# Attention of a hybrid decoder layer as one hand-ordered sequence, with the softmax factors applied to the products and the sums of the down weights moved behind later tiles

## The chip, the core and the metric

One Trainium2 chip, one NeuronCore. The metric is the device time of the whole program in microseconds (us). Engines are TensorE (PE; its weight loads are shown as PEld), VectorE (DVE), ScalarE (ACT), GpSimd (POOL) and SyncE (SP), which here issues all DMAs. Every engine takes its instructions in the order of its own program; a semaphore wait holds back all that is queued behind it on that engine.

## The reference, cut to what matters

A layer of a decoder trunk: T = 1024 tokens, 1024 channels, float32. One input projection feeds three groups of heads (convolution, sparse attention, RWKV-7). Their outputs are concatenated, projected and added to the residual; a gated MLP with a short convolution follows. The change lies in attention, which for 8 query heads (2 groups g of 4 heads r) sums three softmax branches with a sigmoid gate for each. With 16 blocks in all and the best 16 chosen, the selected branch is causal attention over all keys.

```python
def masked_softmax(s, mask, axes):
    s = jnp.where(mask, s, NEG_INF)
    m = jnp.max(s, axis=axes, keepdims=True)
    e = jnp.where(mask, jnp.exp(s - m), 0.0)
    return e / jnp.maximum(jnp.sum(e, axis=axes, keepdims=True), TINY)
...
        o_cmp = jnp.einsum('bgrqn,bngd->bqgrd', pc.astype(v_cmp.dtype), v_cmp)
        o_sel = jnp.einsum('bgrqnl,bgqnld->bqgrd', ps.astype(vg.dtype), vg)
        o_win = jnp.einsum('bgrqk,bkgd->bqgrd', pw.astype(vwc.dtype), vwc)
        return gc[..., 0:1] * o_cmp + gc[..., 1:2] * o_sel + gc[..., 2:3] * o_win
```

## The kernel before

**Stages.** The program normalises x, transposes it, projects it in the three groups, runs convolution, RWKV and attention, then the output projection (out_tile), the MLP's first half (ffn_up) and its second (ffn_down), both as Strassen-like products of half matrices. The code is traced in program order, and a planner that models times then fixes the order of every engine's instructions ahead of the run: of those that are ready it takes the one with the highest priority, which is program order, except that the RWKV steps (start, solve, chain in build) are raised far above all else. Tiles of one tag share a fixed number of buffers (table B, line 23 on), and a tile waits until its buffer is free.

**RWKV.** Four units (j, h), j a pair of heads and h half of the tokens. For each, rwkv_prep and rwkv_mats make the operands and solve a triangular system by substitution on GpSimd, 31 dependent steps of two instructions (L528, L530); rwkv_solve finishes the inverse on TensorE, and rwkv_chain walks over eight chunks with the state (L591, L596, L609, L611) and ends with a store to the DRAM buffer md (L638). The order is "... S10 C01 V10 S11 C10 V11 C11": the operands of unit 11 are made after the solve of unit 10 and the chain of unit 11 is last. Units 10 and 11 fall beside attention.

**Attention.** Query tiles of 128 tokens in the order 7, 6, 5, 4, 0, 3, 2, 1 (attn_tile, L821). For each: loads of Q through SP; scores against the compressed keys (L839), their softmax with two GpSimd steps (L849, L857); then for branch 2 (window, W = up to 640 keys) and branch 1 (selected, W = (i+1) * 128) and for each of four heads r a unit of work, for both groups g:

- score products in pieces of up to 512 keys into PSUM banks of the tag mm, 3 of them (L893, L894: high and low part of the keys);
- a VectorE instruction that adds the mask, copies to SBUF (tile pp) and finds the minimum of the negated scores (L897); L902 joins the minima of two pieces;
- exponential with sums on ScalarE (L904), reciprocal of the sum (L905), times the gate (L906), and the scaling of the probabilities by that factor on VectorE (L911, two for each unit);
- transposes of 128 x 128 blocks into a bank of the tag tr, four blocks or, at the odd end, two (L918), a ScalarE copy to SBUF (pT, L921), and AV products into halves of 64 columns of the array (L926). All three branches accumulate into one bank (av), which L932 copies out and L933 stores.

A pp buffer holds 1280 columns (pk=1280): one unit of 640 keys, both groups, takes one of six buffers; units of more keys take two.

**Sums of down weights.** down_sums(f) (L936) loads four 128 x 512 blocks of w_down, forms four differences on GpSimd (L945 to L948) and stores them for ffn_down. It is called for 11 values of f behind the tiles, two a tile, with nothing to hold the instructions to that place.

**Behind attention.** wout_load (L954) brings w_out in 16 blocks, split into high and low parts; most of the buffers for it are those that RWKV and the keys leave. out_tile(i) (L977) loads two mixed tiles from md (L984; the first holds the convolution and RWKV channels, the second those of attention), splits them (L120, L121) and makes 2 x 24 products (L229), from tile 7 down to tile 0.

## Time and profile before

| what | value |
|---|---|
| median of three runs | 1516.3 us (1515.09 to 1518.08) |
| profiled execution | 1516.71 us, of it 1515.0 us span between first and last instruction |
| granted TensorE clock, mean | 0.962 |
| TensorE busy | 1418.2 us of the span (94%) |
| VectorE, ScalarE, GpSimd busy | 1001.0, 684.0, 500.2 us |
| attention, first score product to last copy | about 400 to 733 us |

The profile is one execution. A duration of a TensorE instruction includes its way through the array, and instructions overlap, so what one costs in a row of others is read from the distance of starts. A wait is put down to the instruction that came last. The views used are the table of stretches, the waits, the list of groups by line, the instructions of one line, and the timeline.

### The profile page before, as it was taken

The numbers are of one execution on the slowest core, as the hardware profiler recorded it, in microseconds if no ns is written. First come the engines' busy times: TensorE is split into PE (matmuls) and PEld (weight loads), VectorE is DVE, ScalarE is ACT, GpSimd is POOL, SyncE is SP. The second block draws the span as 40 slices with busy tenths as digits, with TensorE's granted clock in tenths as the row PEclk, the third lists the DMA queues.
The fourth block names the chain that finished last, engine by engine and source line by source line (L and its number), as shares of the span: only waits on it lengthen the run. The fifth ranks groups of instructions, "written<-read, shape, count | busy, mean of one in ns | idle before, by whom it ended". The sixth has DMA issues, their size and how long they took to land.

```text
span 1515.0 us, 22973 instructions
## 1 busy us (share of the span) xinstructions
PE 1418.2 (94%) x8025; PEld 1128.7 (75%) x8025; DVE 1001.0 (66%) x2171; ACT 684.0 (45%) x1361; POOL 500.2 (33%) x607
## 2 busy tenths in 40 slices
PE   6999688999798999999599899999999999999997
PEld 5887566777666777767478677888888788888886
DVE  5346696454488587777446776775876876666675
ACT  5432255534155665776333353333333443445463
POOL 1003887910487204100000133453453443113310
PEclk9999887999699999999899999999999999999999
DMA  6133223434888301310742113332332333986633
GB/s 184 36 105 80 46 77 95 146 89 119 246 259 270 101 21 41 81 43 16 226 121 84 57 56 98 105 112 84 104 119 91 104 104 111 383 295 213 207 91 111
DMA packets 206680, 186.71 MB, mean 123 GB/s; under 512 B 56355, under 2 KB 145764, under 8 KB 206564
## 3 DMA queue, kind: packets, MB, share of 16 engines
q1 hardware_dynamic: 206564, 185.24, 39.5%
q8 instruction: 63, 1.03, 0.3%
q14 instruction: 53, 0.43, 0.1%
HBM read 126.99 MB, written 58.20 MB: 122 GB/s over the span
## 4 chain that ended last, share of the span: by engine, by line
PE 78%; DVE 10%; DMA 4%; POOL 2%; issue 2%; ACT 2%; SPq 1%; DVEq 0%; ACTq 0%; POOLq 0%
PE mm L229 13%; PE gb L229 12%; PE rw L229 10%; PE ga L229 8%; PE gc L229 8%; PE tr L229 5%; PE tr L918 4%; PE av L926 4%; PE mm L893 2%; PE mm L894 2%; POOL sx L528 1%; PE rw L493 1%; POOL sT L530 1%; DVE pp L897 1%; DVE pp L911 1%
## 5 line engine op out<-in xcount | busy, mean ns | idle before, releaser
L229 PE MATMUL mm<-hT,whi 128*128 128x512 f32 x608 | 201.6, 413 | 0.0
L229 PE MATMUL mm<-hT,wlo 128*128 128x512 f32 x304 | 126.1, 416 | 18.8 <-DVE wlo L121 18.8
L229 PEld LDWEIGHTS mm<-hT,whi 128*128 128x128 f32 x608 | 118.3, 197 | 28.5 <-issue 1.4
L921 ACT ACTIVATE pT<-tr 128x512 f32<-128x512 f32 (+1 forms) x152 | 79.8, 536 | 62.1 <-PE tr L918 59.0
L926 PE MATMUL av<-pT,V 128*64 128x128 f32 x1056 | 96.4, 289 | 1.3 <-ACT pT L921 1.1
L279 POOL TENSOR_TENSOR cacc<-cacc,ctap 128x512 f32<-128x512 f32 x60 | 91.6, 1550 | 15.0 <-ACT ctap L278 14.9
L229 PE MATMUL rw<-woh,mix 128*128 128x512 f32 x240 | 79.4, 406 | 17.0 <-ACT mix L120 17.0
L918 PE MATMUL tr<-idn,pp 128*128 128x128 f32 x528 | 91.6, 292 | 0.5 <-DVE pp L911 0.3
L121 DVE TENSOR_TENSOR sp<-rb,sp 128x512 fp32r<-128x512 f32 x66 | 57.1, 865 | 50.4 <-ACT sp L120 50.3
L1072 POOL TENSOR_TENSOR S<-wraw,wr 128x512 f32<-128x512 f32 x22 | 28.5, 1295 | 181.0 <-DVE or L107 79.2
L229 PEld LDWEIGHTS mm<-hT,wlo 128*128 128x128 f32 x304 | 59.9, 197 | 37.0 <-DVE wlo L121 20.1
L893 PE MATMUL mm<-KH,QS 128*128 128x512 f32 (+2 forms) x192 | 77.3, 407 | 10.0 <-DVE mx L897 7.7
L229 PE MATMUL rw<-sp,sp 128*128 128x512 f32 x330 | 86.1, 389 | 0.0
L229 PE MATMUL tr<-sp,sp 128*128 128x512 f32 x330 | 85.9, 389 | 0.0
L926 PEld LDWEIGHTS av<-pT,V 128*64 128x64 f32 x1056 | 59.9, 138 | 27.3 <-issue 13.0
L528 POOL TENSOR_TENSOR sx<-sN,sT 128x60 f32<-128x60 f32 (+24 forms) x124 | 47.4, 382 | 97.4 <-DMA sN<-dn 90.5
L918 PEld LDWEIGHTS tr<-idn,pp 128*128 128x128 f32 x528 | 56.5, 142 | 30.0 <-issue 27.9
L120 ACT ACTIVATE sp<-rb 128x512 fp32r<-128x512 f32 x66 | 41.6, 630 | 74.0 <-PE tr L229 37.5
L121 DVE TENSOR_TENSOR sp<-b,sp 128x512 fp32r<-128x512 f32 x88 | 68.8, 789 | 5.3 <-ACT sp L120 5.1
L229 PEld LDWEIGHTS rw<-sp,sp 128*128 128x128 f32 x330 | 62.0, 188 | 12.8
L229 PEld LDWEIGHTS tr<-sp,sp 128*128 128x128 f32 x330 | 62.0, 188 | 12.8
L904 ACT ACTIVATE pp<-pp,nm 128x640 f32<-128x640 f32 (+3 forms) x64 | 57.6, 904 | 23.7 <-DVE nm L902 22.1
(457 smaller groups left out, 3721.0 us busy)
## 6 DMA issues: line engine op xcount, KB each, us to landing
wraw<-in_ffn_w_up_dram SPq DMA_DIRECT2D x44, 256.0 KB
wr<-in_ffn_w_gate_dram SPq DMA_DIRECT2D x44, 256.0 KB
pdS<-prod SPq DMA_DIRECT2D x44, 256.0 KB
b<-pdS SPq DMA_DIRECT2D x44, 256.0 KB
rb<-tdT SPq DMA_DIRECT2D x44, 256.0 KB
pdA<-prod SPq DMA_DIRECT2D x33, 256.0 KB
b<-pdA SPq DMA_DIRECT2D x33, 256.0 KB
wraw<-in_w_in_dram SPq DMA_DIRECT2D x30, 256.0 KB
```

The source lines that it names most:

```text
L120: self.nc.scalar.activation(hi, src, AF.Copy)
L121: getattr(self.nc, eng).tensor_tensor(lo, src, hi.bitcast(F32), op=ALU.subtract)
L229: mm = lambda l, r, **k: self.nc.tensor.matmul(out, l, r, skip_group_check=more, **k)
L279: nc.gpsimd.tensor_tensor(t[:, o:o + 512], t[:, o:o + 512], z, op=ALU.add)
L528: v_.tensor_tensor(x, N[:, q, q + 1:32].unsqueeze(2).to_broadcast([P, n, w]), Tm[:, q, 0:w].unsqueeze(1).to_broadcast([P, n, w]), op=ALU.mult)
L893: pe.matmul(pts[g][:, 0:n], QS[:, r, g, :], KH[g][hf][:, ks], start=True, stop=False)
L894: pe.matmul(pts[g][:, 0:n], QS[:, r, g, :], KL[g][hf][:, ks], start=False, stop=True)
L904: s.activation(Ps[g], Ps[g], AF.Exp, bias=nm[:, g:g + 1], scale=-1.0, accum_out=sm[:, g:g + 1])
L918: pe.transpose(pt[:, o:o + P], Ps[g][:, kt * P:kt * P + P], self.idn)
L921: s.activation(pT[:, 0:n], pt[:, 0:n], AF.Copy)
L926: pe.matmul(av[g * 64:g * 64 + 64, r * P:r * P + P], self.V[kk // 2][:, kk % 2, vo + g * 64:vo + g * 64 + 64], pT[:, o:o + P], start=first ...
L1072: gp.tensor_tensor(t, x, y, op=op)
```

## The change

Attention of all tiles becomes one function (attention) that writes out TensorE's order. self.pe gives each attention instruction of TensorE an ordering edge, without a semaphore, to the one before it, so that the planner keeps them in that order; instructions of other parts may still come between them. Work goes in rounds of two items. An item is four transposes of blocks that may belong to two units ("k"), the transposes of the compressed probabilities ("c"), or those of the factors ("f"). A round is: the transposes of its items with their copies, the AV products of the round before, the end of a branch where one is due, scores of the next round's units, scores of the units of the round after that while pp buffers are left, and the compressed AV product.

The probabilities stay unscaled. When all four units of a branch have their sums, attn_factors makes gate over sum for 128 x 8 values, copies each over 64 columns, four transposes bring that into the layout of the products, and VectorE multiplies the branch's products by it (out of the av bank) and adds them to a sum in SBUF that begins with the compressed branch's product. The compressed branch has a bank of its own (mm). Every fourth pT copy is made by VectorE (dvc=4).

There are 9 pT buffers instead of 5. A pp buffer holds 1024 columns instead of 1280, so that a unit of 640 keys takes two. down_sums are called when a tile is opened (its first scores are issued), 0, 3, 2, 3, 2, 1, 0, 0 of them, and their GpSimd instructions are ordered behind the last GpSimd step (formerly L857) of that tile's compressed branch.

```diff
-                      QS=2, pp=6, q8=2, pT=5, xn=8, ds=((0, 1), (2, 3), (4, 5), (6, 7), (8, 9), (10,), (), ()), h2=14, graw=2, prod=5, ft=4, u=4, wr2=4, wfh=3, wfl=3, S=2, p1=2, om=6, grow=2, pre=2, ap=(), wf=("own", "wf", "om"), hd=("vector",) * 4, tq=((0, 1, 2, 3),), ttag=("tr", "rw"),
-                      mm=3, tr=2, av=1, rw=2, mm1=2, tr1=2, pm=2, early="00 01", ga=2, gb=1, gc=1, y=16, r4=15, ta=3, tb=4, mid=2, de=dict(S3="gpsimd", T3="vector", T1="gpsimd", T2="gpsimd", T4="vector", S1="gpsimd", S2="gpsimd", S4="gpsimd"), order=(7, 6, 5, 4, 0, 3, 2, 1), sc=0, pk=1280, st="sync", last=5, sub="gpsimd",  steps="lora r0 S00 conv taps V00 S01 keys q C00 V01 r1a cmp0 r1b cmp1 r1c S10 C01 V10 S11 C10 V11 C11", both=0, cm="gpsimd", rpu=(), wo="vector", tap=(0, 31), vt="cv", vs="vector", va={1: (0, 1), 3: (2, 3), 5: (4, 5), 7: (6, 7)}, vq="sync", vl=1, vw=1, t1=("pm", "tr1"), into={6: (6, 2), 4: (4, 2), 3: (3, 1), 2: (2, 1), 1: (1, 1), 0: (0, 1)})
+                      QS=2, pp=6, q8=2, pT=9, dvc=4, xn=8, ds=((), (0, 1, 2), (3, 4), (5, 6, 7), (8, 9), (10,), (), ()), h2=14, graw=2, prod=5, ft=4, u=4, wr2=4, wfh=3, wfl=3, S=2, p1=2, om=6, grow=2, pre=2, ap=(), wf=("own", "wf", "om"), hd=("vector",) * 4, tq=((0, 1, 2, 3),), ttag=("tr", "rw"),
+                      mm=3, tr=2, av=1, rw=2, mm1=2, tr1=2, pm=2, early="00 01", ga=2, gb=1, gc=1, y=16, r4=15, ta=3, tb=4, mid=2, de=dict(S3="gpsimd", T3="vector", T1="gpsimd", T2="gpsimd", T4="vector", S1="gpsimd", S2="gpsimd", S4="gpsimd"), order=(7, 6, 5, 4, 0, 3, 2, 1), sc=0, pk=1024, st="sync", last=5, sub="gpsimd",  steps="lora r0 S00 conv taps V00 S01 keys q C00 V01 r1a cmp0 r1b cmp1 r1c S10 C01 V10 S11 C10 V11 C11", both=0, cm="gpsimd", rpu=(), wo="vector", tap=(0, 31), vt="cv", vs="vector", va={1: (0, 1), 3: (2, 3), 5: (4, 5), 7: (6, 7)}, vq="sync", vl=1, vw=1, t1=("pm", "tr1"), into={6: (6, 2), 4: (4, 2), 3: (3, 1), 2: (2, 1), 1: (1, 1), 0: (0, 1)})
...
-        cm.tensor_tensor(C4, C4, each(sm), op=ALU.mult)
+        self.cm_ins = cm.tensor_tensor(C4, C4, each(sm), op=ALU.mult).ins
...
+    def pe(self, *a, transpose=False, **k):
+
+        ins = (self.nc.tensor.transpose if transpose else self.nc.tensor.matmul)(*a, **k)
+        if self.pe_last is not None:
+            self.tc.add_manual_dep(ins.ins, self.pe_last.name, mybir.DependencyInfo(mybir.DependencyClass.NoSync, mybir.DependencyReason.DATA),
+                                   reason="attention")
+        self.pe_last = ins.ins
+        return ins
...
-                v.reciprocal(sm, sm)
-                v.tensor_tensor(sm, sm, gt[:, r:8:4, br], op=ALU.mult)
-                for g in range(2):
-                    if g < self.B["sc"]:
-                        s.activation(Ps[g], Ps[g], AF.Copy, scale=sm[:, g:g + 1])
-                    else:
-                        v.tensor_scalar(Ps[g], Ps[g], sm[:, g:g + 1], None, op0=ALU.mult)
...
+    def attn_T(self, x, units):
+
+        pt = self.bank("tr")
+        y = [(units[n], kt, g) for n, kt in x for g in range(2)]
+        for n, (u, kt, g) in enumerate(y):
+            self.pe(pt[:, n * P:n * P + P], u.Ps[g][:, kt * P:kt * P + P], self.idn, transpose=True)
+        pT = self.xt([P, 512], "pT")
+        self.ncopy += 1
+        if self.B["dvc"] and self.ncopy % self.B["dvc"] == 0:
+            self.nc.vector.tensor_copy(pT, pt)
+        else:
+            self.nc.scalar.activation(pT, pt, AF.Copy)
+        return [(*z, pT[:, n * P:n * P + P]) for n, z in enumerate(y)]
+
+    def attn_factors(self, t, br):
+
+        nc = self.nc
+        F = t.sums[br]
+        nc.vector.reciprocal(F, F)
+        f2 = F.rearrange("p (r g) -> p g r", g=2)
+        nc.vector.tensor_tensor(f2, f2, t.gt[:, :, br].rearrange("p (g r) -> p g r", g=2), op=ALU.mult)
+        X = self.xt([P, 512], "pT", name="fx")
+        nc.vector.tensor_copy(X.rearrange("p (a b) -> p a b", b=64), F.unsqueeze(2).to_broadcast([P, 8, 64]))
+        t.X[br] = X
...
+    def attention(self, order, done_tile):
...
+                rounds += [items[k:k + 2] for k in range(0, len(items), 2)]
+        rounds.append([("f", len(units) - 1)])
+
+        top = [max([u for z, x in it if z == "k" for u, _ in x], default=-1) for it in rounds]
...
+        def cmp_av(t):
+            cav = self.bank("mm")
+            self.pe(cav, self.vcmp[0:t.n2], t.ct[0:t.n2], start=True, stop=True)
+            t.mix = self.xt([P, 512], "pT", name="mix")
+            s.activation(t.mix, cav, AF.Copy)
+
+        def fac_T(t, br):
+            pt = self.bank("tr")
+            for r in range(4):
+                self.pe(pt[:, r * P:r * P + P], t.X[br][:, r * P:r * P + P], self.idn, transpose=True)
+            t.fs = self.xt([P, 512], "pT", name="fs")
+            s.activation(t.fs, pt, AF.Copy)
+
+        def end(t, br):
+            v.tensor_tensor(t.fs, t.av, t.fs, op=ALU.mult)
+            v.tensor_tensor(t.mix, t.mix, t.fs, op=ALU.add)
+            if br == 1:
+                self.st.dma_start(self.md[:, 4:8, t.i * P:t.i * P + P], t.mix.rearrange("p (r q) -> p r q", q=P))
+        issue(top[1])
+        late = []
+        for k, items in enumerate(rounds):
...
+            self.attn_AV(late)
+            late = done
+            for u in fs:
+                end(u.t, u.br)
+            far = top[min(k + 2, len(rounds) - 1)]
+            near = top[min(k + 1, len(rounds) - 1)]
+            issue(near)
+            while opened[0] <= far and used() + (1 if 2 * units[opened[0]].w * P <= self.B["pk"] else 2) <= self.B["pp"]:
+                issue(opened[0])
+            for t in cs:
+                cmp_av(t)
...
-        for n, i in enumerate(order):
-            self.attn_tile(i)
-            for f in self.B["ds"][n]:
-                self.down_sums(f)
+        ds = iter(self.B["ds"])
+
+        def done_tile():
+            for f in next(ds):
+                with self.tc.issue_after(self.cm_ins):
+                    self.down_sums(f)
+        self.attention(order, done_tile)
```

## Rows read from the trace of the kernel before

**Rows 1.** Table of stretches: us, each engine's busy us (instructions), granted clock, DMA share, GB/s.

```profile
400.00:500.00 100.00, 89.09 (x656) 65.65 (x657) 79.12 (x231) 50.04 (x100) 78.18 (x106) 0.90 0.83 262
500.00:613.00 113.00, 112.53 (x1051) 85.63 (x1050) 82.11 (x292) 72.59 (x153) 26.66 (x74) 1.00 0.15 39
613.00:733.00 120.00, 117.58 (x1106) 86.15 (x1105) 88.08 (x370) 86.13 (x228) 4.32 (x8) 1.00 0.20 53
...
740.00:750.00 10.00, 3.03 (x7) 2.48 (x8) 2.08 (x3) 2.44 (x4) 0.00 (x0) 0.50 1.04 329
```

**Rows 2.** TensorE's waits from 400 to 500: who waits for whom: us, times, longest.

```profile
PE mm L893 <- DVE mx L897: 7.4, 6, 2.5
```

**Rows 3.** Instructions of L528 (404:504, 585:612) and L596 (500:733): ns min/median/max, first and last start.

```profile
L528 POOL TENSOR_TENSOR sx<-sN,sT x31: 202/289/730, 404.7 to 502.3; 128x60 f32<-128x60 f32 x3, 128x28 f32<-128x28 f32 x2, 128x54 f32<-128x54 f32 x2, 128x48 f32<-128x48 f32 x2
...
L528 POOL TENSOR_TENSOR sx<-sN,sT x31: 203/285/428, 585.9 to 610.4; 128x60 f32<-128x60 f32 x3, 128x28 f32<-128x28 f32 x2, 128x54 f32<-128x54 f32 x2, 128x48 f32<-128x48 f32 x2
...
L596 PE MATMUL rw<-VA,KB x30: 269/273/276, 590.9 to 716.0; 128*128 128x128 f32 x30
```

**Rows 4.** Timeline of GpSimd from 404 us: start, us, line, form, [idle before].

```profile
407.26 1.29 POOL L945 TENSOR_TENSOR wraw<-whi,wraw 128x512 f32<-128x512 f32 x1 [0.39 <-DVE mx L897]
408.51 0.26 POOL L530 TENSOR_TENSOR sT<-sT,sx 128x28 f32<-128x28 f32 x1
408.72 1.28 POOL L946 TENSOR_TENSOR whi<-wlo,whi 128x512 f32<-128x512 f32 x1
```

**Rows 5.** Timelines of SP's queue and of TensorE behind attention.

```profile
736.02 0.43 SPq L638 DMA_DIRECT2D md<-gz  x1
...
741.14 0.43 SPq L984 DMA_DIRECT2D mix<-md  x1
...
746.97 0.80 PE L229 MATMUL rw<-woh,mix 128*128 128x512 f32 x1 [13.32 <-ACT mix L120]
...
764.18 0.50 PE L229 MATMUL rw<-woh,mix 128*128 128x512 f32 x1 [2.48 <-ACT mix L120]
```

**Rows 6.** Timeline of TensorE, 600 to 608 us; neighbours of one line are merged.

```profile
601.01 0.39 PE L894 MATMUL mm<-KL,QS 128*128 128x512 f32 x1
601.24 0.28 PE L893 MATMUL mm<-KH,QS 128*128 128x256 f32 x1
...
605.98 0.44 PE L918 MATMUL tr<-idn,pp 128*128 128x128 f32 x2
606.34 0.66 PE L926 MATMUL av<-pT,V 128*64 128x128 f32 x8
606.93 0.66 PE L918 MATMUL tr<-idn,pp 128*128 128x128 f32 x4
607.34 0.37 PE L893 MATMUL mm<-KH,QS 128*128 128x256 f32 x1
```

**Rows 7.** Groups by line, 400 to 733: count, busy us, mean ns, idle before.

```profile
L921 ACT ACTIVATE pT<-tr 128x512 f32<-128x512 f32 (+1 forms) x152 | 79.8, 536 | 62.1 <-PE tr L918 59.0 <-issue 1.8
L911 DVE TENSOR_SCALAR pp<-pp,sm 128x640 f32<-128x640 f32 (+7 forms) x128 | 66.6, 562 | 1.3
L906 DVE TENSOR_TENSOR sm<-sm,gates 128x2 f32<-128x2 f32 x64 | 13.8, 216 | 1.2
L905 DVE RECIPROCAL sm<-sm 128x2 f32<-128x2 f32 x64 | 10.2, 160 | 17.1 <-ACT pp L904 16.8
```

**Rows 8.** Instructions of L443 and L447, RWKV steps like those the change adds.

```profile
L443 DVE COPY cum<-rrn x4: 419/423/426, 105.0 to 556.6; 128x512 f32<-128x512 f32 x4
...
L447 DVE TENSOR_TENSOR lw<-lw,rw x2: 679/684/689, 378.1 to 560.7; 128x512 f32<-128x512 f32 x2
```

**Rows 9.** VectorE's groups by line and shape, 415 to 500 and 510 to 580.

```profile
L902 DVE TENSOR_TENSOR nm<-mx 128x2 f32<-128x2 f32 x13 | 6.0, 460 | 0.1
...
L902 DVE TENSOR_TENSOR nm<-mx 128x2 f32<-128x2 f32 x10 | 1.5, 155 | 0.1
```

**Rows 10.** Groups by line and shape, 400 to 733, VectorE and ScalarE.

```profile
L897 DVE CUSTOM_DVE_ANT_0 pp<-mm,msel 128x512 f32<-128x512 f32 x48 | 32.3, 685 | 7.7 <-PE mm L894 6.0 <-PE tr L918 1.3
...
L904 ACT ACTIVATE pp<-pp,nm 128x1024 f32<-128x1024 f32 x8 | 9.1, 1142 | 4.7 <-DVE nm L902 4.7
L904 ACT ACTIVATION_READ_ACCUMULATOR pp<-pp,nm 128x1 f32 x64 | 12.2, 190 | 0.0
```

More of the change, by code (lines that the diff above doesn't have):

```diff
@@ new lines, in attn_open @@
+        self.cm_ins = cm.tensor_tensor(C4, C4, each(sm), op=ALU.mult).ins
+        t.X = {}
+        t.sums = [None] + [self.small([P, 8], "sums", bufs=6) for _ in range(2)]
+        return t
+    def pe(self, *a, transpose=False, **k):
[5 more added lines that the diff above has]
+        return ins
@@ new lines, in attn_scores, with mask, piece @@
+    def attn_scores(self, u):
+        v, s = self.nc.vector, self.nc.scalar
+        t, br, r = u.t, u.br, u.r
+        k1 = (t.i + 1) * P
+        lo_k = u.lo_k = max(0, k1 - 640) if br == 2 else 0
+        M = self.mwin if br == 2 else self.msel
+        W = u.W = k1 - lo_k
+        KH, KL = self.KH[br - 1], self.KL[br - 1]
+        pcs = [(a, b) for a, b in ((lo_k, min(k1, 512)), (max(lo_k, 512), k1)) if a < b]
+        npc = len(pcs)
+        mx = self.small([P, 2, npc], f"mx{npc}", bufs=6)
+        if 2 * W <= self.B["pk"]:
+            Pt = self.xt([P, 2, W], "pp")
+            Ps = u.Ps = [Pt[:, g, :] for g in range(2)]
+        else:
+            Ps = u.Ps = [self.xt([P, W], "pp") for _ in range(2)]
+        def mask(ka, kb):
+            e = 640 - (k1 - kb)
+            return M[:, e - (kb - ka):e] if br == 2 or kb == k1 else M[:, 0:kb - ka]
+        def piece(c):
+            ka, kb = pcs[c]
+            hf, n = ka // 512, max(kb - ka, 256)
+            o = min(ka % 512, 512 - n)
+            ks = slice(o, o + n)
+            pts = [self.bank("mm") for _ in range(2)]
+            for g in range(2):
+                self.pe(pts[g][:, 0:n], t.QS[:, r, g, :], KH[g][hf][:, ks], start=True, stop=False)
+                self.pe(pts[g][:, 0:n], t.QS[:, r, g, :], KL[g][hf][:, ks], start=False, stop=True)
+            o = ka % 512 - o
+            for g in range(2):
+                v.tensor_tensor_reduce(Ps[g][:, ka - lo_k:kb - lo_k], pts[g][:, o:o + kb - ka], mask(ka, kb), 1.0, 3.4e38,
+                                       ALU.add, ALU.min, mx[:, g, c:c + 1])
+            if c == npc - 1:
@@ L929, in attn_tile @@
-            if br == 2:
-                cmp_av()
-        mf = self.xt([P, 512], "pT", name="mix")
-        s.activation(mf, av, AF.Copy)
-        self.st.dma_start(self.md[:, 4:8, i * P:i * P + P], mf.rearrange("p (r q) -> p r q", q=P))
+                    s.activation(Ps[g], Ps[g], AF.Exp, bias=nm[:, g:g + 1], scale=-1.0, accum_out=t.sums[br][:, 2 * r + g:2 * r + g + 1])
+        return [lambda c=c: piece(c) for c in range(npc)]
+    def attn_T(self, x, units):
[7 more added lines that the diff above has]
+            self.nc.vector.tensor_copy(pT, pt)
+        else:
+            self.nc.scalar.activation(pT, pt, AF.Copy)
+        return [(*z, pT[:, n * P:n * P + P]) for n, z in enumerate(y)]
@@ new lines, in attn_factors, with attn_AV @@
+    def attn_factors(self, t, br):
[7 more added lines that the diff above has]
+        t.X[br] = X
+    def attn_AV(self, done):
+        for u, kt, g, pT in done:
+            t, r = u.t, u.r
+            if r == 0 and kt == 0 and g == 0:
+                t.av = self.bank("av")
+                t.first = [True, True]
+            vo = 128 if u.br == 2 else 0
+            kk = u.lo_k // P + kt
+            self.pe(t.av[g * 64:g * 64 + 64, r * P:r * P + P], self.V[kk // 2][:, kk % 2, vo + g * 64:vo + g * 64 + 64], pT,
+                    start=t.first[g], stop=r == 3 and kt == u.w - 1)
+            t.first[g] = False
```

137 lines of the change are left out of this document (73 added, 64 removed).

## The prediction, made before the changed kernel was run

> **What bounds the kernel now.** I read the table of stretches first, for where TensorE is short of work, then its waits, then GpSimd's rows and the timeline around the end of attention. Attention runs from 400 to 733 us, with what is left of the RWKV group between its instructions. From 500 to 613 TensorE is busy 112.5 us of 113, from 613 to 733 117.6 of 120, both at the full clock [rows 1]: there the order is limited by TensorE's own work. Only the first 100 us are loose: TensorE is idle for 10.9 us and its granted clock is 0.90 [rows 1], so another tenth of the time runs short, 10 us. Some 20 us are lost there. The largest wait of that stretch is for VectorE's masked copy of the scores (L897), 7.4 us [rows 2].
>
> The second thing to see is GpSimd. The serial solve of the third RWKV unit (31 steps of L528 and L530) runs from 404.7 to 503 us; the next one, with nothing beside it, from 585.9 to 611, that is 25 us [rows 3]. The difference of 73 us is down_sums: 44 subtractions of 1.28 us that take turns with the steps, one 1.29 us subtraction between two steps of 0.26 us [rows 4]. So the RWKV chain, which is serial through solve, products and the next solve, goes on to a last state product at 716.0 us [rows 3].
>
> The third is the seam behind attention. The RWKV result is stored at 736.0 us, the load of the first mixed tile, which needs it, is issued at 741.1, and TensorE starts the output projection at 747.0 after 13.3 us of idleness [rows 5]; the clock is then at the lower of its two levels (1.2 GHz, 0.50 granted from 740 to 750) [rows 1]. With 2.5 us of idleness at 764.2 [rows 5] and about 8 us of products at half speed (4 us lost) I put the seam at 13.3 + 2.5 + 4 = 20 us. So the end of attention and the end of RWKV coincide today, and both must move for a gain.
>
> **The change part by part.** *TensorE's work.* In the timeline eight AV instructions take 606.34 to 606.93, 74 ns each; four transposes 606.93 to 607.34, 103 ns each; but two transposes ahead of an AV group take 0.36 us, 0.15 more than two of 103 ns [rows 6]. So I charge 0.15 us for each visit to the AV products, which use half of the array's columns. Before there are at most 152 visits, one per pT copy [rows 7]. After it, the loop makes 83 rounds (counted from order, the widths w and two items a round) with one visit each: 69 x 0.15 = 10 us less. Added are 16 x 4 = 64 transposes of the factors, 64 x 0.103 = 6.6 us; the transposes and AV products themselves stay. Net -3 us.
>
> *VectorE.* Scaling of the probabilities (L911, 66.6 us) goes; 64 small reciprocals and products (10.2 and 13.8 us) become 16 each [rows 7], 18 us less. Added for each of 16 tile branches: a broadcast copy of 0.42, a product from PSUM of 0.68 and an addition of about the same [rows 8], 16 x 1.8 = 29 us, and every fourth pT copy, 33 x about 0.68 = 22 us (no such copy is in the trace; the nearest row is the PSUM product; the copy of 0.42 is the other end, 14 us). Net -67 - 18 + 29 + 22 = -34 us. *ScalarE:* 152 copies (79.8 us) [rows 7] become 99 plus 16 of the factors, at 0.54 us 62 us, so -18. Neither bounds 500 to 733 us, so these count only where TensorE waits for them: in the first 100 us. There L911 alone is more than the largest wait, and GpSimd's queue no longer puts subtractions ahead of the first tile's compressed scores. I take half of the 20 us, -10; the ends are 0 and -20.
>
> *The sums.* None is issued on GpSimd before the second tile is opened; then 3, 2, 3, 2, 1 follow the tiles, each 4 x 1.28 = 5.1 us [rows 4]. The 44 instructions, their loads and stores on SP's queue stay the same in number. The solve at 404.7 should take about 25 us, so it ends near 430 instead of 503; what follows it in the chain moves with it by up to 73 us. A sum that is queued ahead of a step of the last solve delays it by 1.28 us; the three sums of one tile could cost it 15 us. Both leave the RWKV end before 700 us, hidden behind attention; without that cover the seam comes back. Then the first mixed tiles can be loaded early, w_out finds its buffers, and the output projection follows attention without a gap: -20 us; ends 0 and -20. SP's loads of Q for the next tile now stand behind stores that wait for the sums; a tile lasts some 40 us and three sums 15, so I cost it at nothing.
>
> *The held order.* This is what is paid. A unit's scores are issued one round of transposes and products ahead of their use: 8 x 0.103 + 16 x 0.074 + 0.15 = 2.2 us of cover, more where the round holds other scores. A unit of 1024 keys needs eight score products of 0.23 us [rows 6], and from the last of them: a masked copy of 0.69, the minimum of 0.16 to 0.46 us [rows 9], and two exponentials of 1.14 + 0.19 on ScalarE, one after the other [rows 10], with hand-overs about 4 us. So 4 - 2.2 - 0.4 (first item of the next round) = 1.4 us stay open. For the 12 units of 768 keys and more this is 16 us; for the 20 of 640 keys, whose round holds the next unit's scores (1.4 us), about 0.3, 6 us. The smallest tile (four units a round, all buffers full, so nothing ahead) I put at 2 us in each of four rounds, 8; the other small tiles at 8, the wait for the one AV bank and the compressed branch at 6. Together 44 us if nothing fills it. The RWKV products and the first output products, which are not in the held order, do fill it. The trace does not show how they would fall, so the ends are 5 and 44; I take half, 22.
>
> *A rule against it.* The minimum over two pieces (L902), a two-column VectorE instruction, takes 0.460 us in 415 to 500, with GpSimd busy, and 0.155 us in 510 to 580, where it is mostly idle [rows 9]. The Trainium skill ("SBUF — State Buffer", section "Who interferes with whom") says that VectorE and GpSimd take a shared port pair in turn, for a whole instruction. The sums spread over tiles 6 to 3 take that with them, and there L902 now stands in the chain for which TensorE waits. By the rows 24 units x 0.3 us, with GpSimd busy for a third of the time, is 2.4 us; without the rule 0. It lies within the 22 us and does not change the sum.
>
> **Sum.** -3 - 10 - 20 + 22 = -11 us, and I take 4 us more off for output products that fill the waits of the last tiles (two banks of 24 products of 0.23 us could give 11): -15. The profiled execution took 1516.7 us (span 1515.0), 0.4 over the median of the runs; forecast **1502 us**. Behind the seam all stays as it is.
>
> **The rivals.** *The held order starves TensorE (slower).* Place: tiles 7 to 4, where two-slot units leave three in flight. Price: nothing fills, 44 us, and small waits lower the clock as in the first 100 us, where 10.9 us of idleness went with a tenth less clock [rows 1], so up to 30 more: -3 - 10 - 20 + (44 to 74) = +11 to +41, 1528 to 1558. It decides from 33 us of waiting on. For it: today's order has six units of 640 keys in flight and needs them for 99% busy; against it: VectorE's and ScalarE's chain is shorter. The Trainium skill ("TensorE: Matmul & The Clock Gate", "HAM oscillation — how this bites in real kernels") has the same mechanism, clock lost to repeated waiting; rows 1 agree in the first stretch.
>
> *The sums return the solve's delay.* GpSimd's turns fall on the last solve and the RWKV end stays at attention's end; the seam stays: -3 - 10 + 22 = +9, with half of the seam -1: 1514 to 1526. For it: 5 of 11 sums are issued while that solve would run. Against: 15 us of them against 73 gained.
>
> *The waits are filled nearly everywhere.* -3 - 20 - 20 + 5 = -38, and to -25 with the smaller start gain: 1478 to 1490. For it: RWKV work is spread over the same stretch and is not bound to the order.
>
> **How the numbers follow.** Forecast (1490 to 1514) 0.50; filled 0.18; solve delayed 0.09, about half of it within 0.2% (3 us, about what a measurement of this kernel can tell from no change) and most of the rest slower; starved 0.23. Faster 0.68, same 0.08, slower 0.24. The range takes in the filled case and the lower end of the starved one: 1478 to 1532.
>
> **What would show it.** In the changed profile: the third solve's L528 and L530 within about 30 us of 405; the last RWKV result stored before 700; no wait of 13 us ahead of the first output product; VectorE some 34 us less busy from 400 to 733. TensorE waiting for ScalarE's exponentials ahead of the transposes is the price; over 33 us of it and the forecast is wrong. It is also wrong if the solve stays long, or the seam stays with RWKV done.

## The result, and the profile after

The changed kernel takes 1568.7 us (median of four runs, 1558.7 to 1574.1) against 1517.2 for the kernel before: 1.033 times as long, interval 1.0304 to 1.0358. The profiled execution took 1566.81 us, of it 1565.1 us span, at a mean granted clock of 0.946 (before 0.962).

All of it arises in attention and the output projection. The first product of ffn_up is a mark that every kernel here has. In TensorE's timeline of the kernel before (columns as in [rows 6]) it is:

```profile
864.63 0.78 PE L229 MATMUL gc<-T,whi 128*128 128x512 f32 x1
```

and in that of the changed kernel:

```profile
914.57 0.78 PE L229 MATMUL gc<-T,whi 128*128 128x512 f32 x1
```

It comes 49.9 us later, and the span is 50.1 us longer. The table of stretches up to that mark (columns as in [rows 1]), first of before:

```profile
400.00:864.63 464.63, 429.20 (x3294) 325.08 (x3295) 324.64 (x1078) 248.70 (x577) 115.59 (x192) 0.96 0.39 117
```

and of the changed kernel, whole and by stretch:

```profile
400.00:500.00 100.00, 87.80 (x758) 66.77 (x758) 57.13 (x187) 46.79 (x90) 28.96 (x73) 0.92 0.24 62
500.00:613.00 113.00, 102.53 (x831) 81.06 (x828) 66.46 (x189) 44.65 (x88) 40.51 (x81) 0.83 0.36 107
613.00:733.00 120.00, 107.15 (x833) 81.65 (x833) 77.21 (x254) 62.66 (x153) 35.78 (x31) 0.93 0.50 152
733.00:807.00 74.00, 66.67 (x507) 51.35 (x507) 45.61 (x136) 49.87 (x127) 3.11 (x5) 0.93 0.25 72
...
400.00:914.57 514.57, 460.56 (x3354) 358.61 (x3353) 312.01 (x935) 235.36 (x540) 112.21 (x192) 0.91 0.35 105
```

What to see: TensorE is idle for 514.57 - 460.56 = 54.0 us instead of 35.4, and its granted clock is 0.91 instead of 0.96. A clock of 0.91 over 514.57 us is 46.3 us of full speed not had, 0.96 over 464.63 us is 18.6. So the 49.9 us are 18.6 of idleness, 27.7 of clock, and 3.6 that is left. The clock has two digits, so each of its terms is good to 2.5 us, and it is counted over the idle time too. The stretch 500 to 613, which was full at clock 1.00 [rows 1], now has 102.5 us busy at 0.83.

The sums did what they were moved for. Instructions of L528 (third and fourth solve), of L596, and SP's timeline at the last RWKV store:

```profile
L528 POOL TENSOR_TENSOR sx<-sN,sT x31: 204/278/317, 403.5 to 427.1; 128x60 f32<-128x60 f32 x3, 128x28 f32<-128x28 f32 x2, 128x54 f32<-128x54 f32 x2, 128x48 f32<-128x48 f32 x2
...
L528 POOL TENSOR_TENSOR sx<-sN,sT x31: 203/278/702, 526.6 to 549.4; 128x60 f32<-128x60 f32 x3, 128x28 f32<-128x28 f32 x2, 128x54 f32<-128x54 f32 x2, 128x48 f32<-128x48 f32 x2
...
L596 PE MATMUL rw<-VA,KB x44: 270/275/377, 411.8 to 644.2; 128*128 128x128 f32 x44
```

```profile
669.96 0.33 SPq L638 DMA_DIRECT2D md<-gz  x1
```

The third solve takes 24 us instead of 98 [rows 3], the last state product comes at 644 instead of 716 [rows 3], and the result is stored at 670 instead of 736 [rows 5]. The seam's first wait is gone, and output products begin inside attention, as TensorE's timeline shows:

```profile
722.93 0.40 PE L229 MATMUL rw<-woh,mix 128*128 128x512 f32 x1
```

TensorE's largest waits from 400 to 800 (columns as in [rows 2]):

```profile
PE mm L866 <- DVE mx L908: 8.2, 8, 3.3
PE tr L866 <- ACT pT L930: 6.0, 6, 1.6
PE mm L866 <- ACT pT L1018: 5.8, 3, 2.8
PE tr L866 <- ACT pp L916: 3.6, 8, 0.7
```

and from 733 to 915:

```profile
PE rw L229 <- DVE xn L1124: 6.8, 1, 6.8
```

No wait dominates: the loss is many waits of about a microsecond, and the clock that falls beside them. (All of attention's products have line 866, that of the helper that adds the edges; L908 is the masked copy, L914 the minimum, L916 the exponential, L930 the copy of transposes.)

### The profile page after: what moved, and what is told of

The parts are those of the page before. It is cut to its first block, busy times and chain, and to the rows that moved or that the text cites. A ratio compares the mean times of both kernels' runs of the same rounds, so it can differ in the third digit from the quotient of the medians.

```text
span 1565.1 us, 22869 instructions
## 1 busy us (share of the span) xinstructions
PE 1450.6 (93%) x8089; PEld 1162.9 (74%) x8089; DVE 992.6 (63%) x2028; ACT 670.6 (43%) x1324; POOL 496.4 (32%) x607
## 4 chain that ended last, share of the span: by engine, by line
PE 75%; DVE 11%; DMA 3%; POOL 3%; issue 3%; ACT 3%; SPq 1%; DVEq 0%; POOLq 0%; ACTq 0%
PE mm L229 12%; PE gb L229 12%; PE rw L229 10%; PE ga L229 8%; PE gc L229 8%; PE tr L229 5%; PE mm L866 4%; PE tr L866 4%; PE av L866 3%; PE rw L493 1%; ACT pp L916 1%; DVE pp L908 1%; POOL sx L528 1%; POOL sT L530 1%; DVE cacc L272 1%
## 5 line engine op out<-in xcount | busy, mean ns | idle before, releaser
L866 PE MATMUL tr<-idn,pp 128*128 128x128 f32 x528 | 86.8, 297 | 14.7 <-ACT pT L930 5.8
L866 PEld LDWEIGHTS tr<-idn,pp 128*128 128x128 f32 x528 | 65.6, 151 | 32.0 <-ACT pp L916 9.4
L930 ACT ACTIVATE pT<-tr 128x512 f32<-128x512 f32 x99 | 57.3, 591 | 70.9 <-PE tr L866 70.5
L866 PE MATMUL av<-pT,V 128*64 128x128 f32 x1056 | 86.3, 301 | 0.0
L121 DVE TENSOR_TENSOR sp<-b,sp 128x512 fp32r<-128x512 f32 x88 | 73.0, 839 | 4.8 <-ACT sp L120 4.7
L866 PEld LDWEIGHTS av<-pT,V 128*64 128x64 f32 x1056 | 63.5, 148 | 16.9 <-issue 15.9
L908 DVE CUSTOM_DVE_ANT_0 pp<-mm,msel 128x512 f32<-128x512 f32 (+3 forms) x96 | 49.9, 553 | 37.7 <-PE mm L866 37.4
L916 ACT ACTIVATE pp<-pp,nm 128x640 f32<-128x640 f32 (+3 forms) x64 | 57.5, 901 | 30.7 <-DVE nm L914 29.6
```

Source lines behind the costliest of these rows:

```text
L121: getattr(self.nc, eng).tensor_tensor(lo, src, hi.bitcast(F32), op=ALU.subtract)
L866: ins = (self.nc.tensor.transpose if transpose else self.nc.tensor.matmul)(*a, **k)
L908: v.tensor_tensor_reduce(Ps[g][:, ka - lo_k:kb - lo_k], pts[g][:, o:o + kb - ka], mask(ka, kb), 1.0, 3.4e38, ALU.add, ALU.min, mx[:, g, c: ...
L916: s.activation(Ps[g], Ps[g], AF.Exp, bias=nm[:, g:g + 1], scale=-1.0, accum_out=t.sums[br][:, 2 * r + g:2 * r + g + 1])
L930: self.nc.scalar.activation(pT, pt, AF.Copy)
```

## The experiments

Theories. **A:** the held order itself: score products stand too late in it, or too rigidly. **B:** the late subtractions on GpSimd stretch VectorE's work beside attention. **C:** buffers: too few units in flight, edges or not. **D:** attention in rounds, with factors on the products, costs time by itself. The ratio is to runs of the kernel before that were made along with that run, so it can differ a little from the ratio of the medians shown. The time to the mark, idle us and clock are TensorE's from 400 us to the mark in each kernel's own profile, which is one execution: that of e9 took 1526.9 us, the shortest of its four, and those of e10 (1509.3), e11 (1558.3) and e14 (1520.9) lie above their medians.

| run | edit | median us | ratio to before (interval) | to the mark, us | idle | clock |
|---|---|---|---|---|---|---|
| before | | 1517.2 | 1 | 464.6 | 35.4 | 0.96 |
| after | | 1568.7 | 1.0331 (1.0304 to 1.0358) | 514.6 | 54.0 | 0.91 |
| e1 | after, no edges | 1511.3 | 0.9962 (0.9941 to 0.9982) | 459.0 | 23.2 | 0.97 |
| e5 | after, no edges on scores | 1509.5 | 0.9945 (0.9923 to 0.9968) | 457.1 | 29.8 | 0.96 |
| e6 | after, scores up to 3 rounds ahead | 1541.0 | 1.0142 (1.0103 to 1.0181) | 487.1 | 52.4 | 0.94 |
| e9 | after, up to 8 rounds ahead | 1531.8 | 1.0102 (1.0069 to 1.0135) | 475.5 | 42.3 | 0.97 |
| e2 | before, late sums | 1505.2 | 0.9945 (0.9918 to 0.9973) | 454.0 | 20.7 | 0.96 |
| e3 | after, early sums | 1552.0 | 1.0235 (1.0203 to 1.0266) | 498.7 | 55.8 | 0.93 |
| e4 | after, no subtractions | 1558.4 | 1.0273 (1.0232 to 1.0313) | 505.0 | 46.2 | 0.91 |
| e10 | e5, buffers of 1280 | 1505.6 | 0.9930 (0.9902 to 0.9957) | 457.4 | 33.9 | 0.97 |
| e11 | e9, buffers of 1280 | 1551.3 | 1.0213 (1.0162 to 1.0264) | 506.5 | 58.3 | 0.93 |
| e12 | e1, buffers of 1280 | 1523.3 | 1.0037 (1.0011 to 1.0064) | 468.6 | 29.9 | 0.96 |

**e1: no edges.** Everything else of the change stays.

```diff
-        if self.pe_last is not None:
-            self.tc.add_manual_dep(ins.ins, self.pe_last.name, ...)
-        self.pe_last = ins.ins
```

> The changed kernel without the ordering edges between attention's TensorE instructions; rounds, factors on the products, nine pT and six smaller pp buffers and the late sums stay. Theory A (the held order starves TensorE, and its short waits lower the clock): most of the 50 us come back, 1500 to 1525 us, granted clock from 400 us on near 0.97. Theory B (the late subtractions on GpSimd stretch VectorE's instructions, for which TensorE waits): little comes back, 1550 to 1570. Theory C (three units in flight and scores issued one round ahead are the limit with or without edges): 1545 to 1570.

The loss is gone: 57 us less than the changed kernel, 0.4% (0.2 to 0.6) faster than before. The edges are the cause of the whole slowdown: the rewritten attention (D), its buffers (C) and the late subtractions (B) all stay here, and without the edges none of them brings a loss.

**e5: edges on transposes, AV products and factors, none on scores.**

```diff
-                self.pe(pts[g][:, 0:n], t.QS[:, r, g, :], KH[g][hf][:, ks], start=True, stop=False)
+                self.nc.tensor.matmul(pts[g][:, 0:n], t.QS[:, r, g, :], KH[g][hf][:, ks], start=True, stop=False)
...
```

> The changed kernel with the ordering edges kept among transposes, AV products and factor steps, but none on the score products and the compressed scores, which the planner may place as early as buffers allow. Theory A1 (the order starves TensorE because scores stand too late in it): most comes back, 1505 to 1530 us. Theory A2 (it is the fixed place of transposes and AV products against RWKV's raised work that leaves gaps): 1545 to 1570.

As fast as with no edges. So the edges on the score products (those of the compressed scores among them) carry all of it. In its table of stretches 500 to 613 is nearly full again:

```profile
500.00:613.00 113.00, 110.05 (x961) 89.22 (x960) 85.27 (x277) 61.85 (x125) 46.88 (x87) 0.97 0.45 135
...
400.00:857.06 457.06, 427.29 (x3359) 339.84 (x3359) 305.43 (x937) 234.87 (x540) 112.09 (x192) 0.96 0.39 120
```

Against this run the changed kernel reaches the mark 57.5 us later: 54.0 - 29.8 = 24.2 of idleness, 46.3 - 18.3 = 28.0 of clock, 5.3 left.

**e6 and e9: the edges stay, scores stand earlier in the order.**

```diff
-            far = top[min(k + 2, len(rounds) - 1)]
+            far = top[min(k + 3, len(rounds) - 1)]
```

(e9: k + 8.)

> The changed kernel, all edges kept, but scores opened up to three rounds ahead instead of two, where the six pp buffers allow it (units of 768 keys and more then get one more round of cover, 2.2 us). Theory A1: a part comes back, 10 to 30 us, 1540 to 1560. Theory A2: within 8 us of the changed kernel, 1560 to 1575.

> Every ordering edge is kept; scores are opened up to eight rounds ahead instead of two (the run before opened three), which is as far as the six buffers of 1024 columns ever allow. If lookahead in the order is all that is missing, this goes on from 1541 us to 1510 to 1530, with 500 to 613 us again at a granted clock over 0.95. If three rounds are already all that six buffers hold, it repeats 1541 us (1535 to 1547), and the rest of the loss is that the order has no place for work that is ready while it waits. If scores far ahead take the three banks of mm from the pieces that are needed next, it gets slower than 1541.

One round more gives back 28 us, and as many rounds as the buffers hold another 9. The two tables of stretches, e6 first:

```profile
500.00:613.00 113.00, 100.21 (x938) 81.13 (x939) 67.11 (x213) 49.23 (x98) 29.89 (x73) 0.94 0.25 70
```

```profile
500.00:613.00 113.00, 108.09 (x1029) 87.74 (x1029) 74.82 (x241) 57.03 (x116) 45.51 (x87) 0.98 0.36 109
```

With e9 the clock is back (0.98 here, 0.97 up to the mark). Most of what e9 regains up to the mark is clock: 46.3 - 14.3 = 32.0 us, beside 54.0 - 42.3 = 11.7 of idleness. The lookahead is 37 of the 59 us between the medians of the changed kernel and e5; 22 stay with one shared sequence as far ahead as six buffers let it look. In the profiles e9's mark is 18.4 us behind e5's, of which 12.5 are idleness (42.3 against 29.8) and none is clock; the rest is not accounted for, and why these 22 us stay is open. e9 ended between the band for "lookahead is all" (1510 to 1530) and that for "buffers end it" (1535 to 1547).

**e11 and e13: the edges and the buffers.** e11 is e9 with score buffers of 1280 columns (a unit of 640 keys takes one) and seven copy buffers; e13 has the seven copy buffers alone.

```diff
-                      QS=2, pp=6, q8=2, pT=9, dvc=4, ...
+                      QS=2, pp=6, q8=2, pT=7, dvc=4, ...
...
-                      ... sc=0, pk=1024, ...
+                      ... sc=0, pk=1280, ...
```

> Every ordering edge is kept, scores are opened up to eight rounds ahead (that run: 1531.8 us), and the buffers are those of the kernel before: 1280 columns, so that six units of 640 keys are in flight instead of three; seven copy buffers instead of nine. If what is left of the loss, 22 us against the run with free scores, comes from too few units in flight, this falls to 1505 to 1518. If it comes from the order itself (a score product whose bank or buffer isn't free yet stands in front of transposes that are ready), it stays at 1525 to 1540.

> The held order with scores up to eight rounds ahead (1531.8 us), and of the buffers only the copies of the transposes reduced from nine to seven; those of the scores stay at 1024 columns. The run with both changed took 1551.3. If the copy buffers made the 19 us, this is 1545 to 1557 too. If the wider score buffers did, because scores far ahead then stand in front of transposes that are ready, this stays at 1528 to 1537.

e11 was a miss: slower by 20 us with more units in flight. e13 took 1535.8 us (ratio 1.0117, 1.0085 to 1.0148), within the interval of e9, so it was the wider score buffers. C falls: with the order held, room for more units in flight costs 15 us. Without edges on scores the same two sizes make no difference clear of noise (e10, below: 4 us the other way), but without any edges they cost 12 us (e12, below), so the loss with wide buffers does not belong to the held order alone. That scores which stand early in the sequence block transposes that are ready would fit e11, but no row here shows it, and it stays an argument.

**e3 and e4: the sums under the held order.** e3 puts the sums where they were before the change, two a tile with nothing to hold them. e4 leaves out the four subtractions of each of the 11 sums, so the sums of down weights are not formed; their loads and stores stay.

```diff
...
-                with self.tc.issue_after(self.cm_ins):
-                    self.down_sums(f)
+                self.down_sums(f)
```

> The changed kernel with the sums as before (two a tile, behind the tile, no ordering on GpSimd). Theory A: attention stays starved, the third solve is long again and RWKV's work lies elsewhere: 1555 to 1590 us. Theory B: the stretching moves back to the first 100 us, 1525 to 1545.

> The changed kernel without the 44 subtractions of the sums on GpSimd: the loaded blocks are stored as they are, loads and stores stay (this part of the computation is left out). Theory A: the subtractions were a side matter, 1545 to 1565 us. Theory B: VectorE's instructions take their usual time and TensorE waits less, 1515 to 1540.

Without any subtraction the kernel is about 10 us faster and its clock up to the mark still 0.91: B is worth about 10 us. e3 is the odd one: alone the late sums gain 8 to 12 us (e2, next), under the held order they cost 15 to 17. In its table of stretches the first 100 us show the old trouble, subtractions beside the solve, worse than in [rows 1]:

```profile
400.00:500.00 100.00, 77.37 (x568) 58.00 (x568) 54.42 (x158) 37.59 (x71) 73.31 (x109) 0.86 0.82 255
500.00:613.00 113.00, 105.51 (x965) 83.35 (x965) 74.04 (x239) 57.46 (x114) 24.14 (x68) 0.92 0.16 47
```

What it wins comes after 500 us (clock 0.92 against 0.83), where GpSimd is busy 24.1 us instead of 40.5. But e4, with 21.0 us of GpSimd in the same stretch, has 0.86 there, so the subtractions alone don't explain it; how much is the changed place of the RWKV work stays open.

**e2: the late sums alone, on the kernel before.**

```diff
...
+        cm_ins = cm.tensor_tensor(C4, C4, each(sm), op=ALU.mult).ins
+        for f in self.B["ds"][self.B["order"].index(i)]:
+            with self.tc.issue_after(cm_ins):
+                self.down_sums(f)
```

> The kernel before with one part of the change alone: the sums of down weights, 0, 3, 2, 3, 2, 1 of them, ordered on GpSimd behind the last compressed step of a tile. My forecast's reason (the third solve is 73 us shorter, RWKV ends before 700 us, the seam behind attention closes): 1490 to 1505 us. Theory B: what the early stretch gains is paid back where VectorE works beside the sums, 1515 to 1530.

Faster by 0.55% (0.27 to 0.82): 8 us by the ratio, 12 between the medians, 10.7 at the mark. Its eight times are five of 1502.9 to 1505.3 and three of 1512.3 to 1514.4, and the median is in the lower group. Its table of stretches and the timeline of TensorE at the seam:

```profile
400.00:500.00 100.00, 96.67 (x866) 72.56 (x866) 74.66 (x247) 60.96 (x121) 38.04 (x79) 0.96 0.33 93
500.00:613.00 113.00, 109.14 (x870) 82.84 (x868) 84.80 (x290) 60.67 (x127) 47.22 (x86) 0.92 0.37 113
613.00:733.00 120.00, 115.97 (x1045) 82.87 (x1044) 96.63 (x364) 87.01 (x235) 24.78 (x24) 0.98 0.46 145
```

```profile
733.30 0.79 PE L229 MATMUL rw<-woh,mix 128*128 128x512 f32 x1 [0.34 <-ACT mix L120]
...
753.03 0.79 PE L229 MATMUL rw<-woh,mix 128*128 128x512 f32 x1 [5.07 <-DVE xn L997]
```

The first 100 us have 3.3 us of idleness instead of 10.9 and a clock of 0.96 instead of 0.90 [rows 1]; the wait of 13.3 us [rows 5] is 0.34. From 500 to 733 us, where the subtractions stand now, it pays back as much: 5.0 us more of idleness than in [rows 1], and a clock of 0.92 and 0.98 instead of 1.00, 11.4 us. So the rival of this run's expectation holds in part. After the first 48 output products, which fill the two banks, TensorE also waits 5.07 us until the first residual sum frees one. SP's timeline shows why that sum is late:

```profile
746.56 0.37 SPq L936 DMA_DIRECT2D md<-mix  x1
747.99 0.36 SPq L987 DMA_DIRECT2D mix<-md  x1
748.40 4.90 SPq L991 DMA_DIRECT2D xn<-in_x_dram  x8
```

The residual's loads stand in SP's queue behind the store of attention's last result. The same wait is 6.6 to 6.9 us in e1, e5, e6, e7, e9 and the changed kernel.

**e7** put the same sums behind the fourth to sixth tile (4, 4, 3), past the last solve.

> The kernel before with the sums alone moved, as in the earlier run of that kind, but 4, 4 and 3 of them behind the fourth, fifth and sixth tile, so that none stands beside the last RWKV solve. If what the sums cost is the time they take from the solves: 1495 to 1505 us, below the placement of the change. If only the third solve matters: 1503 to 1510, the same as that placement. If sums late in attention delay the w_out loads, whose buffers they share: 1508 to 1520.

It took 1511.7 us (0.9962, 0.9935 to 0.9988): the last solve came down to 24 us (534.2 to 558.4), without a gain over e2 (38 us for that solve, 536.7 to 574.6), so the sums beside the last solve are not what keeps e2 from more.

**e14** moved attention's stores in e2 to ScalarE's queue, to clear SP's. **e15** did so in e10.

```diff
-        self.st.dma_start(self.md[:, 4:8, i * P:i * P + P], ...)
+        nc.scalar.dma_start(self.md[:, 4:8, i * P:i * P + P], ...)
```

> The kernel before with the late sums (1505.2 us), and attention's results are stored through ScalarE's DMA queue, behind the copy that makes them, instead of SP's. In that run a 5.1 us wait of TensorE for the first residual sum stayed in the seam; the residual's load stood in SP's queue behind the store of attention's last result. If that store was the cause, the wait goes and the time is 1498 to 1503. If the wait only moves (the load's own time, or the product banks), it stays at 1503 to 1508.

> Free score products with buffers of 1280 columns (1505.6 us), and attention's results stored through ScalarE's queue. In that run TensorE waited 9.7 us for the first mixed tile, whose load came on SP's queue behind a store that waits for attention's last sum. If the store was the cause, this is 1496 to 1502; if RWKV's end or the load's own time sets the seam, 1502 to 1508.

Both missed: 1512.2 (0.9960, 0.9939 to 0.9981) and 1513.9 (0.9971, 0.9950 to 0.9992). Their intervals overlap those of e2 and e10, so no gain is shown, nor a clear loss. The wait itself did shrink, here in e14:

```profile
PE rw L229 <- DVE xn L997: 1.8, 1, 1.8
```

but the planner makes every engine's order anew. In e14's order RWKV's result is stored at 732.5 (e2: 722.1), mixed tiles are waited for again (3.3 us), and waits for masked copies are 7.6 us (e2: 3.1): 28.8 us of idleness up to the mark instead of 20.7. (This is the longest of e14's twelve executions beside a short one of e2, so the rows show more than the medians differ.) Differences of 5 to 10 us between these variants can't be put down to their edit alone; the 57 and 37 us above are far beyond that.

**e10 and e12: wider score buffers without edges on scores, and without any edges.** Edits as in e11, on e5 and on e1.

> The score products without ordering edges (that run: 1509.5 us), and also the buffers as in the kernel before: 1280 columns each, so that a unit of 640 keys takes one of six; two of the nine copy buffers are given up to make room (7). If units in flight limit what is left of the loss against the kernel before with late sums (1505.2 us), this is 1495 to 1506. If not, it stays at 1506 to 1514; if the nine copy buffers mattered, it is slower than 1514.

> No ordering edge at all (that run: 1511.3 us), with buffers of 1280 columns and seven copy buffers. Factors on the products, rounds as program order, late sums remain. If the narrower buffers were the reason that the rewritten attention is some 6 us slower than the attention before with late sums (1505.2 us), this gives 1500 to 1508; if the rounds themselves are, 1508 to 1515.

e10 has the lowest ratio of all, 0.9930, level with e2 and e5 within the intervals; both e10 and e2 beat both kernels. e12 missed: it is 12 us slower than e1. Its SP timeline shows a part of that:

```profile
722.99 0.33 SPq L638 DMA_DIRECT2D md<-gz  x1
...
725.81 0.49 SPq L1033 DMA_DIRECT2D md<-mix  x1
...
746.38 0.37 SPq L1033 DMA_DIRECT2D md<-mix  x1
747.83 0.45 SPq L1110 DMA_DIRECT2D mix<-md  x1
```

The RWKV result is stored at 723.0 (e1: 704.9). It just misses the place in the queue where mixed tiles could be loaded before the last attention result; the load comes at 747.8 (e1: 709.1), and TensorE waits 9.4 us for it:

```profile
754.18 0.80 PE L229 MATMUL rw<-woh,mix 128*128 128x512 f32 x1 [9.39 <-ACT mix L120]
```

This is not the whole reason: e10 has a wait of the same kind, 9.7 us, and is not slower than e5.

**e8: filling TensorE's waits with work.** One 512-column product without use, ahead of each of 132 groups of transposes, inside the held order, to see whether the clock then falls less.

```diff
+        self.pe(pt, y[0][0].t.QS[:, 0, 0, :], self.KH[0][0][0], start=True, stop=True)
```

> The changed kernel with one more product of 512 columns ahead of each of the 132 groups of transposes, into the bank that the transposes then overwrite (its result is not used): 30 us of work at the full clock, ready before the probabilities are. If half of the loss is clock that falls in the gaps: granted clock from 400 us to the end of attention from 0.90 to 0.96 or more, and the time within 12 us of the changed kernel, 1557 to 1580. If the clock does not hang on the gaps: clock 0.90 as before and 1580 to 1600.

1582.1 us (1.0417, 1.0366 to 1.0467), 13 us more than the changed kernel. The clock rose, in part:

```profile
500.00:613.00 113.00, 98.42 (x814) 76.87 (x813) 68.61 (x198) 42.48 (x83) 40.36 (x80) 0.89 0.38 115
...
400.00:927.88 527.88, 475.46 (x3486) 368.45 (x3485) 314.41 (x935) 235.72 (x540) 112.28 (x192) 0.95 0.34 103
```

0.95 instead of 0.91 up to the mark is 46.3 - 26.4 = 20 us back, idleness stays at 52.4, and the 132 products cost more than the clock returns. So added work gave back part of the clock without less waiting, but at a loss.

## Why the prediction was wrong, point by point

**What failed: "The held order", +22 us.** Against free scores it is 57 us in the profiles (e5 against the changed kernel). Two things were wrong in that term. Halving 44 to 22 rested on "The RWKV products and the first output products, which are not in the held order, do fill it". And the sum had no term for the granted clock. The idleness came out near the sum, 24.2 us against 22, but partly by luck, since the wait that I named was a small one (next point). The other 28.0 us are clock. I had its price in hand, in [rows 1] (10.9 us of idleness with 0.90), and wrote it into the rival alone, "up to 30 more", with a point of decision of 33 us of waiting. It does not begin at 33: it came with 24. With the clock beside the idleness the sum is -15 + 30 = +15, slower, before anything else is corrected. The rival "The held order starves TensorE" named the mechanism; its 1528 to 1558 ended below the result since it credited the whole start and seam gains.

**The other half of the miss is gains that did not come.** All terms but the held order add up to -3 - 10 - 20 - 4 = -37 us. With free scores the mark comes 7.6 us before that of the kernel before. So of the 65 us from -15 to +50, some 35 are the held order and 29 are gains. (The chance of "same", 0.08, is also more than the half of 0.09 that its working gives.)

**The row that should show it was not the one that showed it.** I expected TensorE to wait for exponentials ahead of transposes; that row is 3.6 us. The cover was lost in longer chains. The changed kernel's timelines show one of them from 504 us on. VectorE:

```profile
505.81 1.75 DVE L463 TENSOR_TENSOR lw<-lw,tha 128x512 f32<-128x512 f32 x1
...
508.63 1.82 DVE L469 TENSOR_TENSOR BK<-lw,Pi 128x256 f32<-128x256 f32 x2
510.37 1.23 DVE L914 TENSOR_TENSOR nm<-mx 128x2 f32<-128x2 f32 x1
```

ScalarE:

```profile
511.70 0.83 ACT L916 ACTIVATE pp<-pp,nm 128x640 f32<-128x640 f32 x1 [7.33 <-DVE nm L914]
...
513.34 0.57 ACT L1018 ACTIVATE pT<-tr 112x512 f32<-112x512 f32 x1
```

TensorE, and after it the table of stretches of the same 40 us:

```profile
508.76 2.07 PE L474 MATMUL rw<-cum,bones 128*128 128x512 f32 x2 [1.70 <-DVE cum L472]
510.76 5.65 PE L493 MATMUL rw<-VAc,BK 64*128 64x64 f32 x29
...
519.61 2.07 PE L866 MATMUL mm<-pT,vcmp 112*128 112x512 f32 x2
...
523.94 3.67 PE L493 MATMUL rw<-rP,BK 64*128 64x64 f32 x16
...
529.63 0.80 PE L866 MATMUL mm<-KH,QS 128*128 128x512 f32 x1
```

```profile
500.00:520.00 20.00, 16.56 (x93) 13.44 (x90) 15.68 (x34) 4.14 (x10) 9.23 (x8) 0.62 0.65 203
520.00:540.00 20.00, 20.00 (x116) 15.62 (x116) 6.93 (x18) 7.80 (x14) 10.73 (x35) 0.70 0.34 99
```

RWKV's raised VectorE steps stand in front of the minimum that attention needs; ScalarE has waited 7.33 us for it. The next attention product in the held order is the compressed one (519.61), and the copy that it needs (L1018) stands behind these exponentials on ScalarE. Later scores can't go ahead: the order has them behind that product and the transposes that follow it, and the next ones start at 529.63. So TensorE runs RWKV's products of 64 columns; the compressed product, whose copy is done at 513.9, comes behind them. They keep TensorE busy, but the granted clock stays at the lower of its two levels, 0.50 in each stretch from 506 to 530 us, and is 1.00 again from 532 on. The 40 us of the table lose 20 x 0.38 + 20 x 0.30 = 13.6 us of full speed, of the 46.3 up to the mark. 16 of these products take 3.67 us; before, where the clock was 1.00 (570 to 574 us), they take 2.00 (timeline of TensorE in the kernel before):

```profile
571.77 2.00 PE L493 MATMUL rw<-VAc,BK 64*128 64x64 f32 x16
```

So they do fill the order's holes with busy time, but here at half the clock. And my chain of 4 us from last score to exponential left out other parts' instructions on VectorE.

**The rule on the shared port** works as written, but at 2.4 us I priced the two-column minimum alone. The one above lasted 1.23 us, as a subtraction of 1.26 us ran on GpSimd; in 500 to 580 eight of them averaged 0.29. Larger steps stretch too: L463 above took 1.75 us beside subtractions, 0.685 at its shortest in this trace. The Trainium skill ("SBUF — State Buffer", "Who interferes with whom") gives that turn-taking, and the trace agrees; e4 puts all that the subtractions cost at about 10 us.

**Sums and seam, -20: right in mechanism, about half in size.** In the changed kernel solve, state products and the 13.3 us wait went as written. (The 44 subtractions of 1.28 us are only 56 of the 73 us by which the third solve was longer; the sum did not say what the rest is.) The RWKV result before 700 us came with the held order only: it is stored at 670 there, at 722.1 in e2 and at 706.1 in e5. Alone the sums give 8 to 12 us (e2). Of the 17.0 us that TensorE waited for mixed tiles in the kernel before, 0.3 is left in e2, but 5.1 to 6.9 us came back as the wait for the first residual sum. I had costed SP's queue at nothing by looking at the loads of Q; the queue mattered at the other end, at the store of attention's last result.

**The start, -10: there in the first 100 us, but not in the time.** I gave it to VectorE's lighter work and to GpSimd's queue together. e2, where attention is untouched, has more than all of it: 7.6 us less idleness and a clock of 0.96, 6 us. So it belongs to the sums. But e2 pays it back from 500 to 733 us (16.4 us, its rows above), and my sum had nothing for that. In the changed kernel the first 100 us have 12.2 us of idleness at 0.92.

**VectorE, -34: the parts were nearly right, and it didn't matter.** The groups by line of the changed kernel from 400 to 820 (columns as in [rows 7]):

```profile
L928 DVE COPY pT<-tr 128x512 f32<-128x512 f32 x33 | 22.7, 687 | 11.1 <-PE tr L866 10.8
...
L1035 DVE TENSOR_TENSOR mix<-mix,fs 128x512 f32<-128x512 f32 x16 | 14.1, 881 | 0.1
...
L1034 DVE TENSOR_TENSOR fs<-av,fs 128x512 f32<-128x512 f32 x16 | 11.0, 688 | 15.8 <-PE av L866 12.8 <-ACT fs L1031 2.1 <-ACT pT L930 0.8
...
L941 DVE COPY fx<-sums 128x512 f32<-128x512 f32 x16 | 7.8, 489 | 0.6
```

22.7 for the copies (22 taken), 32.9 for the factors (29), which makes the net of the parts -28 to -29. Up to the mark VectorE is busy 12.6 us less in the changed kernel and 19 to 23 less in e1 and e5 than in before or e2. ScalarE is 13.3 us less (18 forecast). Yet e10, with the lighter VectorE, and e2, without, take the same time: VectorE and ScalarE bound nothing there, as [rows 1] had it. TensorE's net -3 is smaller than what these runs can tell.

## What to carry to other kernels

An order written by hand for an in-order engine must be as deep as the longest chain behind it, other parts' instructions included: count the rounds of lookahead, not the mean work in one. Here one more round gave 28 us and all that the buffers allow 37, and 22 stayed. Where an engine is near 100% busy, give the granted clock a term of its own beside the idleness, and a range for it: against free scores it was 28.0 us beside 24.2 of idleness in the changed kernel, 16.6 beside 26.0 in e3, and nothing beside 12.5 in e9. Before rewriting the work, move the one thing that the profile shows in the way (here the sums), by itself: no run with the rewritten attention is faster than that, clear of noise.

## What the runs showed of the hardware that was not expected

The granted clock fell after short waits and stayed low while TensorE was shown as busy. The changed kernel's table of stretches around the place shown above:

```profile
494.00:504.00 10.00, 6.89 (x58) 5.45 (x58) 10.00 (x28) 3.31 (x8) 6.95 (x6) 1.00 0.69 230
506.00:530.00 24.00, 22.30 (x99) 17.70 (x98) 12.07 (x19) 4.60 (x9) 9.04 (x14) 0.50 0.64 190
```

From 494 to 505 us TensorE waited four times, 0.48, 1.31, 1.48 and 0.26 us, and the clock fell at the end of that. From 510 on TensorE was shown as busy throughout, much of it with products of 64 columns, and the clock was at the lower level until 530; from 532 on it was 1.00. The Trainium skill ("TensorE: Matmul & The Clock Gate", "HAM oscillation — how this bites in real kernels") describes a clock that repeated waits throw back again and again. The trace agrees in that the fall follows waits, but the page's are long DMA waits between bursts of products, and here the longest one before the fall was 1.48 us.

Part of the clock can also be had back at nearly the same idleness: e3, idle 55.8 us, has 0.93; e8, 52.4 us, 0.95; the changed kernel, 54.0 us, 0.91. So idleness alone doesn't give the clock. Which waits and which products lie between them may, but these runs don't settle it.
